# A feed-forward matrix cut into input halves for two blocks at once, and modulation sums moved between TensorE and VectorE

## The chip, the cores and the metric

One core of one Trainium2 chip. The metric is the device time of one execution in microseconds; the kernel before takes 1133.08 us (median of 3 runs, 1132.43 to 1134.42). Engines: TensorE (PE; PEld is its weight load), VectorE (DVE), ScalarE (ACT), GpSimd (POOL), and SP, whose queue issues most DMA loads.

## The reference

One layer of an encoder: 256 tokens, width 2048, float32.

```
mod = silu(c) @ mod_w + mod_b                  # six vectors of 2048: shift, scale, gate, twice
h   = x * (1 + scale_m) + shift_m
y   = windowed attention (32 heads of 64, 8 key heads) of h, then @ w_o
x   = layer_norm(alpha * x + (1 + gate_m) * y)
h   = x * (1 + scale_f) + shift_f
y   = square(relu(h @ w1 + b1)) @ w2 + b2      # w1 is 2048 x 8192, w2 is 8192 x 2048
out = layer_norm(alpha * x + (1 + gate_f) * y)
```

All weights are read once, so 1 MB tiles of weights stream in for the whole time.

## The kernel before

**Stream.** Every weight tile (128x2048) goes through one queue, `S`. `S.plan` appends a tile to the list, `loads` (L182) issues its DMA on SP as soon as one of five buffers (`raw`) is free, and `pump` works the tiles off in the order of the list. A matrix tile is cut into two halves of 128x1024; of each half ScalarE makes a rounded copy `wh` (L218, "high part") and VectorE the rest `wl` (L190, "low part"), five buffers each. TensorE multiplies high by high, high by low and low by high, so that the product has float32 precision from three fast passes (helper `mm3`, L439 to L441, for attention output and second feed-forward matrix).

**Modulation.** A vector of 2048 for one token, `silu(c) @ mod_w`, is a sum over weight tiles ("chunks"). The class `Mod` sums a chunk either on TensorE (`quad`, L274: 16 records for a chunk of a group of four columns, `raw` against `cact`) or on VectorE (L304, L306: two multiply-adds of 128x1024 into a part tile); which chunks go to VectorE is a list given for each `Mod`. At the end `quad` gathers VectorE's part on TensorE (L274 with `onesf`). The feed-forward shift and scale come as four groups of eight chunks, `m_ff` (tensor `modf`): group g serves the columns 512g to 512g + 511 of the feed-forward input. The attention gate is `m_gm`, the feed-forward gate `m_gf` (16 chunks of `modgf`, all on VectorE). `ff_columns(g)` turns a finished group into scale and shift (transposes L326 on TensorE, then small VectorE operations); `ff_input(g)` transposes the normed x (L834), and ScalarE (L840, L843) and VectorE (L846 and, for the low halves, L848) make the input group `h2[g]` of it, 512 rows of the transposed input.

**Order.** Where modulation chunks stand among the matrix tiles is written by hand: `SLOT_FILL` for the attention stage, `S.vecs(4)` at its end, `W1_FILL` among the tiles of the first feed-forward matrix. Within an engine, the order of instructions is chosen when the program is built, from the kernel's text and the free buffers; the engines then run their queues in that order.

**Hand-over.** At the end of attention, `project` makes the last columns of the output, `add_gated` (L688 to L690) adds them to x and collects statistics, `norm_scalars` (L694 to L704, with the square root on ScalarE, L698) and `normed` (L717, L719) apply the layer norm; then `ff_columns(0)`, `S.vecs(4)` and `ff_input(0)`.

**Feed-forward.** The 8192 hidden columns are four blocks (`BLK`). For block 0 the first matrix comes in tiles of 512 input rows by 512 hidden columns (`w1a`), in the order W1A: first the input groups 0 and 1 for all four column groups `fq`, then groups 2 and 3, with half sums parked in `uacc`; so it can start when only group 0 of the input exists. Its matmuls are 128x256 (L904 to L906). For blocks 1 to 3 `ff_hidden` takes a tile with all 2048 input rows for 128 hidden columns (`w1b`), with one 128x512 and one 128x256 matmul for a weight tile (L928, L929). After each block `ff_out` multiplies by the block's rows of the second matrix (`w2`) and adds to `ys`. The tiles of `m_gf` are planned among `w1b` and `w2` of block 1. During block 1, alpha times the norm's gain and bias is worked into x (`xs`), which stays in SBUF throughout. The general pool `gen` has 26 tiles of 128x1024.

Of the kernel before, what the change touches and what calls it, by code (L numbers as in the profile page):

```python
# [11 lines left out]
F32 = mybir.dt.float32  # L12
F32R = mybir.dt.float32r
# [7 lines left out]
S = 256  # L21
# [3 lines left out]
FF = 8192  # L25
# [5 lines left out]
BLK = 4  # L31
MIXG = (2, 4, 4, 4, 2)
FFG = (4, 4, 4, 4)
# [8 lines left out]
def hybrid_kernel(ctx: ExitStack, tc: tile.TileContext, a, out: bass.AP):  # L42
    nc = tc.nc
# [3 lines left out]
    whp = ctx.enter_context(tc.tile_pool(name="whp", bufs=NHIGH))  # L47
    wlp = ctx.enter_context(tc.tile_pool(name="wlp", bufs=NLOW))
    gen = ctx.enter_context(tc.tile_pool(name="gen", bufs=26))
    psa = ctx.enter_context(tc.tile_pool(name="psa", bufs=5, space=PSUM))  # L50
# [199 lines left out]
    S = Stream()  # L250
# [112 lines left out]
    m_gf = Mod([a["modgf"][i] for i in range(NK)], 512, range(NK), a["modgfb"])  # L363

# [12 lines left out]
    for g in range(G):  # L377
        n = MIXG[g] * 6 // 4
# [5 lines left out]
        for x, c in enumerate(chs):  # L384
# [4 lines left out]
            if not g:  # L389
                m_mix[1][0].plan(m)  # L390
            qk_order.append((g, c))
    late = [m_gm] + [m[0] for m in m_ff[:3]]
    lp = [0]

    def plan_late(n):
# [3 lines left out]
            if lp[0] < len(late):  # L399
                late[lp[0]].plan()  # L400

    W1_FILL = [1, 1, 1, 0, 0, 2, 0, 3, 0, 0, 0, 0, 0, 0, 0, 0]
    SLOT_FILL = dict(enumerate([0, 1, 2, 1, 0, 1, 3, 0, 1, 3, 2, 0, 3, 5, 1, 1, 3, 2, 1, 3, 0, 0, 1], -2))
    for n in range(-2, 21):
        plan_late(SLOT_FILL.get(n, 0))
        if n + 2 < len(LATE):
# [3 lines left out]
            S.plan(a["wo"][(n - 5) % 4, (n - 5) // 4])  # L410
    S.stop = len(S.q)
    plan_late(4)
    W1A = [(kg, fq) for p in ((0, 1), (2, 3)) for q in ((0, 1), (2, 3)) for kg in p for fq in q]
    for n, (kg, fq) in enumerate(W1A):
        left = [m.n - m.planned for m, _, _ in m_ff]
        for _ in range(max(W1_FILL[n], left[2] if n == 6 else 0, left[2] + left[3] if n == 8 else 0)):
            m_ff[2 if m_ff[2][0].planned < m_ff[2][0].n else 3][0].plan()
        S.plan(a["w1a"][kg, fq])
    NF = FF // 128 // BLK
    for blk in range(BLK):  # L420
        for f in range(NF):
            if blk:
                if blk == 1 and f % 2:
                    m_gf.plan()
                S.plan(a["w1b"][(blk - 1) * NF + f])
        for c in range(4):
            for kg in range(4):
                if blk == 1 and kg % 2:
                    m_gf.plan()
                S.plan(a["w2"][blk, c, kg], None, blk == BLK - 1 and c == 3 and kg > 1)  # L430


    acc, xts, held, xs = {}, {}, {}, []
# [1 line left out]
    def part(tiles, t, c):  # L435
        return tiles[c][:, t * 512:t * 512 + 512]
# [272 lines left out]
    def normed(c, t):  # L709
        mv, rstd = sc[t]  # L710
        z = part(xs, t, c)
        if t and c == 0:
            nm = sml.tile([128, 1], F32, name="nmr")
            nc.vector.scalar_tensor_tensor(nm, mv[:, 0:1], -1.0, rstd, op0=OP.mult, op1=OP.mult)
            sc.append(nm)
        if t:
            nc.scalar.activation(z, z, AF.Identity, scale=rstd, bias=sc[2])  # L717
        else:
            nc.vector.tensor_scalar(z, z, mv[:, 0:1], rstd, op0=OP.subtract, op1=OP.mult)  # L719
# [131 lines left out]
    def ff_in(k):  # L851

        return h2[k // 4][k % 4 // 2][:, k % 2 * 512:k % 2 * 512 + 512]

    h2 = [ff_input(0)]
    for c in range(1, 4):
        for t in range(NT):
            normed(c, t)


    def square_split(ps, ft, n, u, at):
# [20 lines left out]
        nc.vector.tensor_sub(l, uf, f32(h))  # L882

    g2 = None
    uacc = [g4() for _ in range(4)]
    us = []
    opened = {}
    for n, (kg, fq) in enumerate(W1A):
        if n in (1, 7, 9):
            ff_columns(len(h2))  # L890
            h2.append(ff_input(len(h2)))
        wh, wl = S.main()
        for fp in range(2):
            if kg % 2 == 0:
                opened[fq, fp] = psa.tile([128, 512], F32, name="pa")
            ps = opened[fq, fp]
            for fi in range(2):
                o = ps[:, fi * 256:fi * 256 + 256]
                for k in range(4):
                    w = (fp * 2 + fi) * 4 + k  # L900
                    hb = ff_in(4 * kg + k)
                    hh, hl = hb[:, :256], hb[:, 256:]
                    new, end = kg % 2 == 0 and fi + k == 0, kg % 2 == 1 and fi == 1 and k == 3
                    nc.tensor.matmul(o, wh(w, 128), hh, start=new, stop=False)  # L904
                    nc.tensor.matmul(o, wh(w, 128), hl, start=False, stop=False)  # L905
                    nc.tensor.matmul(o, wl(w, 128), hh, start=False, stop=end)  # L906
            S.done()
            av = uacc[fq][:, fp * 512:fp * 512 + 512]
            if kg == 1:
                nc.scalar.copy(av, ps)  # L910
            elif kg == 3:
                nc.vector.tensor_add(av, av, ps)
                u = g4(F32R)
                square_split(av, fq * 4 + fp * 2, 2, u, 0)
                us.append(u)

    def ff_hidden(blk):
        nonlocal g2
# [26 lines left out]
    def ff_out(blk, us, c):  # L945
# [6 lines left out]
                S.done()  # L952
        return pss

    ys = [g4() for _ in range(4)]
    bf = bias_all(a["b2"])
    for blk in range(BLK - 1):
        if blk:
            us = ff_hidden(blk)
        for c in range(4):  # L960
            if blk == 1:
                gb = [sml.tile([128, 512], F32, name="gb", tag="t2", bufs=4) for _ in range(2)]
                for n in range(2):
                    nc.gpsimd.dma_start(gb[n], a["lnrow"][n:n + 1, c * 512:c * 512 + 512].partition_broadcast(128))
            for t, ps in enumerate(ff_out(blk, us, c)):
                if blk == 0:
                    nc.vector.tensor_add(part(ys, t, c), ps, bf(c))
                else:
                    nc.vector.tensor_add(part(ys, t, c), part(ys, t, c), ps)
            if blk == 1:  # L970
# [47 lines left out]
def _layout(i):  # L1018
# [43 lines left out]
    n0 = FF // BLK  # L1062
    wa = w1[:, :n0].reshape(4, 4, 128, 4, 4, 128)
    o["w1a"] = cc(wa.transpose(0, 3, 2, 4, 1, 5).reshape(4, 4, 128, 2048))
# [28 lines left out]
```

## Time and profile before

| | before |
|---|---|
| median of 3 runs | 1133.08 us |
| the profiled execution | 1131.72 us, of which the span from first to last instruction is 1130.0 us |
| granted TensorE clock, mean | 0.994 |
| moved by DMA | 288.50 MB |
| hand-over: last matmul of attention to first of the first matrix | 388.18 to 396.64 us |
| first matrix of block 0 | 396.64 to 496.36 us |
| second matrix of block 0 | 496.5 to 583.4 us |
| blocks 1 to 3 | 583.5 us to the end |

All times in rows are microseconds from the start of the span. "L274" is line 274 of the kernel before; a row of the timeline has start, duration, engine, line, operation, output and inputs, shape and count, and in brackets how long the engine stood idle before and what ended it.

### The profile page before, as it was taken

Reading aid. Unit: us, or ns where it says so; the run is one execution under the profiler, and the core shown is the slowest. Engines: PE = TensorE matmul, PEld = TensorE weight load, DVE = VectorE, ACT = ScalarE, POOL = GpSimd, SP = SyncE. Lnnn points to the kernel's source line nnn. Section 1 sums busy time; section 2 is a strip of 40 time slices with the busy share of each in tenths; the row PEclk is TensorE's granted clock in tenths of the full one; section 3 lists DMA queues with packets and bytes.
Section 4 is the critical chain, followed back from the end, with each engine's and each line's share of the span. In section 5 each row is a group of like instructions: output and inputs, shape, how many; then the busy total and the mean of one; then the engine's idle time right before and its main releaser. Section 6 shows DMA issues by size and latency. Waiting matters only on the chain.

```text
span 1130.0 us, 15722 instructions
## 1 busy us (share of the span) xinstructions
PE 1091.6 (97%) x6224; PEld 876.6 (78%) x6224; DVE 810.1 (72%) x1123; ACT 539.3 (48%) x841; POOL 28.9 (3%) x47
## 2 busy tenths in 40 slices
PE   4899999999999999999999999999999999999995
PEld 2566677666676799998888888888888888888884
DVE  5556878987989977865568887966665656665576
ACT  2242345786676264753344543335454334444340
POOL 2000000000000000000000001020000000000001
PEclk9999999999999999999999999999999999999998
DMA  9998988876886599655577788775555557555522
GB/s 349 389 381 327 362 318 324 311 258 250 314 319 234 222 377 368 229 185 194 202 278 282 271 284 306 288 258 204 186 187 190 195 202 269 187 187 186 186 75 75
DMA packets 43866, 288.50 MB, mean 255 GB/s; under 512 B 5232, under 2 KB 7440, under 8 KB 10000
## 3 DMA queue, kind: packets, MB, share of 16 engines
q1 hardware_dynamic: 40640, 279.82, 67.5%
q0 software_dynamic: 2304, 6.36, 1.8%
q10 hardware_dynamic: 848, 1.31, 0.3%
q8 instruction: 49, 0.80, 0.3%
q14 instruction: 25, 0.20, 0.0%
HBM read 285.37 MB, written 2.10 MB: 254 GB/s over the span
## 4 chain that ended last, share of the span: by engine, by line
PE 91%; DVE 4%; DMA 3%; ACT 1%; issue 1%; DVEq 0%; ACTq 0%
PE pa L440 16%; PE pa L441 16%; PE pa L439 16%; PE pa L928 16%; PE pa L929 8%; PE pm L274 4%; PE pa L905 3%; PE pa L904 3%; PE pa L906 3%; DMA raw<-in_wqkv 2%; PE pa L680 2%; PE pt L665 1%; DVE wl L190 1%; PE pa L626 1%; PE pt L594 1%; DVE g L306 1%
## 5 line engine op out<-in xcount | busy, mean ns | idle before, releaser
L190 DVE TENSOR_TENSOR wl<-raw,wh 128x1024 fp32r<-128x1024 f32 x332 | 405.6, 1228 | 219.4 <-ACT wh L218 218.8
L218 ACT CAST wh<-raw 128x1024 fp32r<-128x1024 f32 x332 | 347.7, 1053 | 441.9 <-PE pa L441 232.9
L439 PE MATMUL pa<-wh,g 128*128 128x512 f32 x816 | 322.7, 397 | 4.0 <-ACT wh L218 4.0
L440 PE MATMUL pa<-wl,g 128*128 128x512 f32 x816 | 321.2, 394 | 2.8 <-DVE wl L190 2.8
L441 PE MATMUL pa<-wh,g 128*128 128x512 f32 x816 | 320.4, 393 | 0.0
L928 PE MATMUL pa<-g,wh 128*128 128x512 f32 x768 | 270.1, 396 | 0.0
L929 PE MATMUL pa<-g,wl 128*128 128x256 f32 x768 | 215.5, 281 | 0.0
L439 PEld LDWEIGHTS pa<-wh,g 128*128 128x128 f32 x816 | 153.6, 189 | 45.0 <-issue 6.5
L440 PEld LDWEIGHTS pa<-wl,g 128*128 128x128 f32 x816 | 154.2, 189 | 37.3 <-DVE wl L190 4.4
L441 PEld LDWEIGHTS pa<-wh,g 128*128 128x128 f32 x816 | 154.0, 189 | 35.7 <-issue 3.5
L928 PEld LDWEIGHTS pa<-g,wh 128*128 128x128 f32 x768 | 144.1, 188 | 34.6
L929 PEld LDWEIGHTS pa<-g,wl 128*128 128x128 f32 x768 | 145.1, 189 | 0.2
L306 DVE SCALAR_TENSOR_TENSOR g<-raw,cact,g 128x1024 f32<-128x1024 f32 (+1 forms) x83 | 100.6, 1216 | 9.4 <-DMA raw<-in_modgf 6.2
L905 PE MATMUL pa<-g,wh 128*128 128x256 f32 x256 | 72.7, 285 | 0.4 <-DVE g L848 0.4
L904 PE MATMUL pa<-g,wh 128*128 128x256 f32 x256 | 72.5, 286 | 0.0
L906 PE MATMUL pa<-g,wl 128*128 128x256 f32 x256 | 72.3, 283 | 0.0
L274 PE MATMUL pm<-raw,cact 128*32 128x256 f32 (+2 forms) x800 | 59.2, 406 | 8.9 <-DMA raw<-in_modm 7.9
L904 PEld LDWEIGHTS pa<-g,wh 128*128 128x128 f32 x256 | 48.8, 192 | 1.3 <-issue 0.8
L905 PEld LDWEIGHTS pa<-g,wh 128*128 128x128 f32 x256 | 49.1, 192 | 0.9 <-DVE g L848 0.8
L512 DVE TENSOR_TENSOR g<-g,pa 128x512 f32<-128x512 f32 x44 | 29.8, 682 | 27.0 <-PE pa L441 27.0
L906 PEld LDWEIGHTS pa<-g,wl 128*128 128x128 f32 x256 | 49.1, 192 | 0.0
L274 PEld LDWEIGHTS pm<-raw,cact 128*32 128x32 f32 x800 | 22.6, 114 | 32.7 <-issue 13.8
(169 smaller groups left out, 801.7 us busy)
## 6 DMA issues: line engine op xcount, KB each, us to landing
raw<-in_w SPq DMA_DIRECT2D x64, 1024.0 KB, 5.0
raw<-in_w1b SPq DMA_DIRECT2D x48, 1024.0 KB, 4.9
raw<-in_modm SPq DMA_DIRECT2D x32, 1024.0 KB, 8.1
raw<-in_modf SPq DMA_DIRECT2D x32, 1024.0 KB, 7.1
raw<-in_wqkv SPq DMA_DIRECT2D x24, 1024.0 KB, 7.1
raw<-in_modgm SPq DMA_DIRECT2D x16, 1024.0 KB, 5.3
raw<-in_wo SPq DMA_DIRECT2D x16, 1024.0 KB, 6.9
raw<-in_w1a SPq DMA_DIRECT2D x16, 1024.0 KB, 8.1
```

The lines of the kernel that those rows point to most:

```text
L190: nc.vector.tensor_sub(l, r, f32(self.hs[n]))
L218: nc.scalar.copy(h, s)
L274: nc.tensor.matmul(self.ps[32 * j:32 * j + 32, :w], lhsT, rhs[j], start=self.first, stop=stop)
L306: nc.vector.scalar_tensor_tensor(p[:, :e], s, cact[:, kt:kt + 1], p[:, :e], op0=OP.mult, op1=OP.add)
L439: nc.tensor.matmul(ps, xh, wh, start=start, stop=False)
L440: nc.tensor.matmul(ps, xh, wl, start=False, stop=False)
L441: nc.tensor.matmul(ps, xl, wh, start=False, stop=stop)
L904: nc.tensor.matmul(o, wh(w, 128), hh, start=new, stop=False)
L905: nc.tensor.matmul(o, wh(w, 128), hl, start=False, stop=False)
L906: nc.tensor.matmul(o, wl(w, 128), hh, start=False, stop=end)
L928: nc.tensor.matmul(ps, wh(k, 128), hb, start=k == 0, stop=False)
L929: nc.tensor.matmul(ps[:, :256], wl(k, 128), hb[:, :256], start=False, stop=k == NK - 1)
```

## The change

1. The first matrix of blocks 0 and 1 is now cut by input halves together: `w1a` covers 4096 hidden columns (8 column groups). A first pass does input groups 0 and 1 for all eight, then come groups 2 and 3 for block 0, its second matrix, groups 2 and 3 for block 1, its second matrix. `ff_hidden` remains for blocks 2 and 3.
2. The chunks of `m_ff` that VectorE sums: group 0 from (1, 5, 7) to (1, 4, 6), group 1 from (1, 4, 5, 6) to (0, 1, 2), group 2 from (2) to all, group 3 from (1, 2, 4, 5, 6, 7) to all. The four chunks at the end of attention are now the last of group 1, all on TensorE; groups 2 and 3 are planned within the first pass.
3. x is written to device memory by GpSimd's queue after the norm (`spill`) and read back ahead of the second matrix of block 2, and its four tiles go back to the pool in between; the work on x that stood in block 1 moves to block 2.
4. The bias `b2` comes column by column instead of as two tiles, and the tiles of `m_gf` are planned among `w2` of blocks 0 and 1.

```diff
-    m_ff = groups(a["modf"], FFG, [(1, 5, 7), (1, 4, 5, 6), (2,), (1, 2, 4, 5, 6, 7)])
+    m_ff = groups(a["modf"], FFG, [(1, 4, 6), (0, 1, 2), range(8), range(8)])
...
-    late = [m_gm] + [m[0] for m in m_ff[:3]]
+    late = [m_gm] + [m[0] for m in m_ff[:2]]
...
-    W1_FILL = [1, 1, 1, 0, 0, 2, 0, 3, 0, 0, 0, 0, 0, 0, 0, 0]
-    SLOT_FILL = dict(enumerate([0, 1, 2, 1, 0, 1, 3, 0, 1, 3, 2, 0, 3, 5, 1, 1, 3, 2, 1, 3, 0, 0, 1], -2))
+    SLOT_FILL = dict(enumerate([0, 1, 1, 1, 1, 1, 2, 1, 1, 2, 1, 1, 2, 2, 1, 1, 2, 1, 1, 2, 1, 1, 1], -2))
...
+    W1P = [[(kg, fq) for q in qs for kg in p for fq in (q, q + 1)]
+           for p, qs in [((0, 1), (0, 2, 4, 6)), ((2, 3), (0, 2)), ((2, 3), (4, 6))]]
+    W1_FILL = [0, 0, 1, 1, 1, 2, 1, 2, 1, 1, 2, 1, 1, 1, 1, 0]
+
+    def plan_ff():
+        def first(p):
+            for n, (kg, fq) in enumerate(W1P[p]):
+                for _ in range(0 if p else W1_FILL[n]):
+                    m_ff[2 if m_ff[2][0].planned < m_ff[2][0].n else 3][0].plan()
+                S.plan(a["w1a"][kg, fq])
+
+        def second(blk):
+            for c in range(4):
+                for kg in range(4):
+                    if blk < 2 and kg % 2:
+                        m_gf.plan()
+                    S.plan(a["w2"][blk, c, kg], None, blk == BLK - 1 and c == 3 and kg > 1)
...
+    z_far = far.tile([128, 4096], F32, name="z_far")
+
+    def spill(c):
+        nc.gpsimd.dma_start(z_far[:, c * 1024:c * 1024 + 1024], xs[c])
...
     h2 = [ff_input(0)]
+    spill(0)
     for c in range(1, 4):
         for t in range(NT):
             normed(c, t)
+        spill(c)
...
-    for n, (kg, fq) in enumerate(W1A):
-        if n in (1, 7, 9):
-            ff_columns(len(h2))
-            h2.append(ff_input(len(h2)))
...
+    def ff_first(p):
+        us = []
+        for n, (kg, fq) in enumerate(W1P[p]):
+            if p == 0 and n in (1, 9, 15):
+                ff_columns(len(h2))
+                h2.append(ff_input(len(h2)))
...
+    ff_first(0)
...
-            us = ff_hidden(blk)
+        us = ff_hidden(blk) if blk == 2 else ff_first(1 + blk)
+        if blk == 2:
+            xs = [g4() for _ in range(4)]
+            for c in range(4):
+                nc.gpsimd.dma_start(xs[c], z_far[:, c * 1024:c * 1024 + 1024])
```

The body of `ff_first` is otherwise that of the loop over W1A in before. The layout of `w1` in memory follows.

More of the change, by code (lines that the diff above doesn't have):

```diff
@@ L49, in hybrid_kernel @@
     gen = ctx.enter_context(tc.tile_pool(name="gen", bufs=26))
+    far = ctx.enter_context(tc.tile_pool(name="far", bufs=1, space=bass.MemoryType.DRAM))
     psa = ctx.enter_context(tc.tile_pool(name="psa", bufs=5, space=PSUM))
@@ L412, in hybrid_kernel @@
     plan_late(4)
-    W1A = [(kg, fq) for p in ((0, 1), (2, 3)) for q in ((0, 1), (2, 3)) for kg in p for fq in q]
-    for n, (kg, fq) in enumerate(W1A):
[L415 to L418, printed above, removed]
-    NF = FF // 128 // BLK
[L420 to L430, printed above, removed]
+    NF = FF // 128 // BLK
+    W1P = [[(kg, fq) for q in qs for kg in p for fq in (q, q + 1)]
[13 more added lines that the diff above has]
+                    S.plan(a["w2"][blk, c, kg], None, blk == BLK - 1 and c == 3 and kg > 1)
+        first(0)
+        for blk in range(BLK):
+            if blk < 2:
+                first(1 + blk)
+            else:
+                for f in range(NF):
+                    S.plan(a["w1b"][(blk - 2) * NF + f])
+            second(blk)
+    plan_ff()
     acc, xts, held, xs = {}, {}, {}, []
@@ L884, in hybrid_kernel @@
     g2 = None
[L885 to L888, printed above, removed]
-        if n in (1, 7, 9):
-            ff_columns(len(h2))
-            h2.append(ff_input(len(h2)))
[L892 to L915, printed above, removed]
@@ L1061, in _layout @@
     w1 = f(i["mlp_w1"])[0]
-    n0 = FF // BLK
-    wa = w1[:, :n0].reshape(4, 4, 128, 4, 4, 128)
-    o["w1a"] = cc(wa.transpose(0, 3, 2, 4, 1, 5).reshape(4, 4, 128, 2048))
+    n0 = FF // 2
+    wa = w1[:, :n0].reshape(4, 4, 128, 8, 4, 128)
+    o["w1a"] = cc(wa.transpose(0, 3, 2, 4, 1, 5).reshape(4, 8, 128, 2048))
     wb = w1[:, n0:].reshape(NK, 128, (FF - n0) // 128, 128)
```

43 lines of the change are left out of this document (35 added, 8 removed).

## The prediction

> **What bounds the kernel now.** I read the page first: busy shares, slices, chain.
>
> ```profile
> PE 1091.6 (97%) x6224; PEld 876.6 (78%) x6224; DVE 810.1 (72%) x1123; ACT 539.3 (48%) x841; POOL 28.9 (3%) x47
> ...
> PE   4899999999999999999999999999999999999995
> ...
> PE 91%; DVE 4%; DMA 3%; ACT 1%; issue 1%; DVEq 0%; ACTq 0%
> ```
>
> TensorE is busy in every slice but the ends and holds 91% of the chain. Next, the waits of TensorE: what ended its idle times, with total, count and longest.
>
> ```profile
> PE pm L274 <- DMA raw<-in_modm: 7.9, 2, 7.4
> ...
> PE pa L439 <- ACT wh L218: 4.0, 3, 2.8
> ...
> PE pm L274 <- DMA raw<-in_modf: 1.0, 1, 1.0
> PE pa L905 <- DVE g L848: 0.4, 1, 0.4
> ```
>
> The first two lie at the start and in the projection of the first 160 us, which the change leaves alone. The last two lie at the hand-over from attention to the feed-forward part, and are small. Then windows of the stages that the change touches (columns: stretch, length, busy PE, PEld, DVE, ACT, POOL, granted clock, DMA share, GB/s):
>
> ```profile
> 240.00:260.00 20.00, 20.00 (x101) 13.30 (x101) 19.00 (x35) 17.61 (x44) 0.00 (x0) 1.00 0.70 256
> ...
> 396.50:450.00 53.50, 53.11 (x453) 50.30 (x451) 41.76 (x56) 29.36 (x43) 0.00 (x0) 1.00 0.95 371
> 496.50:583.40 86.90, 86.90 (x386) 71.97 (x385) 49.50 (x49) 35.59 (x36) 0.00 (x0) 1.00 0.62 215
> ...
> 674.00:762.00 88.00, 88.00 (x392) 72.90 (x391) 69.41 (x71) 35.30 (x35) 12.73 (x15) 1.00 0.79 284
> ```
>
> TensorE is full even where VectorE is busy 19.00 of 20 us. So an instruction taken from TensorE here is worth its whole slot, and one that makes TensorE wait costs its whole wait.
>
> **The change, part by part.** First what TensorE saves and gains. The rows give a modulation chunk among matmuls, a group's gather of its VectorE part (L274 from onesf), and the two forms of the first matrix.
>
> ```profile
> 401.70 0.28 PE L906 MATMUL pa<-g,wl 128*128 128x256 f32 x1
> 401.91 1.07 PE L274 MATMUL pm<-raw,cact 128*32 128x256 f32 x16
> 402.91 0.39 PE L904 MATMUL pa<-g,wh 128*128 128x256 f32 x1
> 403.13 0.28 PE L905 MATMUL pa<-g,wh 128*128 128x256 f32 x1
> ...
> 444.66 0.64 PE L274 MATMUL pm<-g,onesf 128*32 128x256 f32 x8
> ...
> 464.19 0.28 PE L905 MATMUL pa<-g,wh 128*128 128x256 f32 x1
> ...
> 488.19 0.28 PE L904 MATMUL pa<-g,wh 128*128 128x256 f32 x1
> ...
> 583.54 0.39 PE L928 MATMUL pa<-g,wh 128*128 128x512 f32 x1
> ...
> 654.19 0.40 PE L928 MATMUL pa<-g,wh 128*128 128x512 f32 x1
> ```
>
> From 464.19 to 488.19 lie 200 matmuls: 0.120 us each. From 401.70 to 403.13 lie two of them and a chunk: 1.43 - 0.24 = 1.19 us. From 583.54 to 654.19 lie 200 pairs (L928, L929): 0.353 us each.
>
> Feed-forward chunks on TensorE fall from 18 (groups 0 to 3: 5, 4, 7, 2) to 10 (5, 5, 0, 0). Where they stand matters. Before stood 11 ahead of the last column of the attention output, 5 at the hand-over, 2 in the first matrix; in the built changed program 6, 4 and none.
>
> - Ahead of the hand-over: five chunks fewer. Alone they cost 1.19; next to transposes, which share the change of form, about the 1.00 from 401.91 to 402.91. I take 1.1: -5.5 us. Group 1's gather moves from here into the hand-over: -0.6. Sum **-6.1** (bounds -5.6, -6.6).
> - In the first matrix: one chunk leaves the part that I count below as hand-over, one the rest (-1.2); the rest has two gathers instead of one (+0.65). Sum **-0.55**.
> - Block 1 by halves: 256 x (3 x 0.120 - 0.353) = **+1.7**.
>
> **The hand-over** is where I differ from "fewer instructions, less time". After the last column of the attention output comes the layer norm, then the first input group; TensorE has only modulation chunks to do. Rows of before, its own clock:
>
> ```profile
> 378.26 0.33 SPq L182 DMA_DIRECT2D raw<-in_w1a  x1
> ...
> 382.74 0.39 PE L441 MATMUL pa<-wh,g 128*128 128x512 f32 x1
> ...
> 383.11 2.00 ACT L218 CAST wh<-raw 128x1024 fp32r<-128x1024 f32 x2 [7.05 <-DMA raw<-in_w1a]
> ...
> 385.13 1.28 ACT L698 ACT_TABLE_LOAD   x1
> ...
> 389.02 0.68 DVE L688 TENSOR_TENSOR tmp<-pa,g 128x512 f32<-128x512 f32 x1
> 389.63 0.68 DVE L690 BATCH_NORM_STATS2 st<-g 128x6 f32<-128x512 f32 x1
> ...
> 391.29 0.20 ACT L698 ACTIVATE sd<-ve 128x1 f32<-128x1 f32 x1 [4.88 <-DVE ve L696]
> ...
> 392.60 0.21 DVE L700 RECIPROCAL r<-sd 128x1 f32<-128x1 f32 x2
> 393.44 0.54 DVE L719 TENSOR_SCALAR g<-g,mv,r 128x512 f32<-128x512 f32 x1
> 394.08 1.52 ACT L717 ACTIVATE g<-g,nmr,r 128x512 f32<-128x512 f32 x2 [1.50 <-DVE nmr L714]
> 395.86 0.57 ACT L840 ACTIVATE g<-pt,b,a 128x256 fp32r<-128x256 f32 x1 [0.25 <-PE pt L834]
> 396.46 0.54 DVE L846 TENSOR_SCALAR g<-pt,a,b 128x256 f32<-128x256 f32 x1 [1.04 <-ACT g L840]
> ...
> 399.58 0.42 DVE L848 TENSOR_TENSOR g<-g,g 128x256 fp32r<-128x256 f32 x1
> ...
> 399.98 0.39 ACT L318 COPY mrow<-pm 128x256 f32<-128x256 f32 x1
> ...
> 415.04 0.28 PE L904 MATMUL pa<-g,wh 128*128 128x256 f32 x1
> ```
>
> In before the first w1a tile is requested at 378.26 and split by ScalarE at 383.11, long ahead of the table load and the square roots. In the built changed program it takes the buffer of the last output-projection tile, and VectorE's low part that frees this buffer has moved ten places back: behind the products of the third column, whose last matmul is that at 382.74. So, aligned there: the column's first half ends six matmuls of 0.353 - 0.120 = 0.23 earlier, at 382.74 + 0.39 - 1.4 = 381.8; from then VectorE does six operations at 0.61 each (389.02 to 389.63), then the low part (1.22), to 386.7; the load goes out, and lands 4.85 later (378.26 to 383.11), 391.55. ScalarE's queue has this tile's cast ahead of table load and roots: 391.55 + 1.05 + 1.28 + 2 x 0.2 = 394.3. The reciprocals start there instead of 392.60. Then ScalarE has group 1's row copy (0.39) and two casts (1.05 each) ahead of its norms, which start at 396.8 instead of 394.08; the first input activation at 398.3 instead of 395.86.
>
> VectorE, the norms done at 396.9, has two low parts ahead of the input group (2.45, to 399.4) and two products of group 2's modulation between its operations. The last low half of the input (399.58 in before) ends at 404.5 instead of 400.0. For what follows these groups are needed (minimum, median, maximum in ns):
>
> ```profile
> L218 ACT CAST wh<-raw x332: 1028/1053/1098, 20.8 to 1093.0; 128x1024 fp32r<-128x1024 f32 x166
> L190 DVE TENSOR_TENSOR wl<-raw,wh x332: 1193/1224/3419, 21.9 to 1094.1; 128x1024 fp32r<-128x1024 f32 x166
> L306 DVE SCALAR_TENSOR_TENSOR g<-raw,cact,g x83: 744/1279/1286, 14.0 to 754.1; 128x1024 f32<-128x1024 f32 x73, 128x512 f32<-128x512 f32 x10
> ```
>
> From 404.5 VectorE's queue holds, up to the last low half of the second input group, six low parts, four modulation products (1.21 each back to back), two 0.54, four 0.42 and six small ones (some 0.1 each, by the reciprocals' 0.21 for two): 7.3 + 4.85 + 1.1 + 1.7 + 0.6 = 15.6, to 420.1. TensorE has 75 matmuls on group 0 left (9.0) and eight transposes (some 0.7, by the gather's 0.64 for eight), is done at 414.3 and waits some 2.5 us. It passes its 124th matmul of the first matrix at 420.2; before passed it at 415.04, with a modulation chunk done besides. **+5.2**. Bounds: +1.7, the delay of the roots alone, if the rest of VectorE's queue finds cover; +8.5, if the load takes the usual 8.1 of this group:
>
> ```profile
> raw<-in_w1a SPq DMA_DIRECT2D x16, 1024.0 KB, 8.1
> ```
>
> **After that.** VectorE in the 16 tiles of the first half-input pass: 32 low parts (39.2), 32 modulation products (38.9), three input groups (3 x (1.1 + 1.7 + 0.6) = 10.2): 88.3 in TensorE's 768 x 0.120 = 92.2 plus some 6 of transposes and gathers. It fits, as in 240 to 260, but the queue is served in order: the shift and scale of group 2 wait for TensorE's transposes, placed at matmul 432, and behind them stand three products, two scalings, two low halves and the low part for half-tile 20. I count 6 + 1.2 us of VectorE against 6.6 of TensorE: **+0.7** (bounds 0, 3).
>
> At nothing I cost: group gf's 16 loads, now in the second matrix of blocks 0 and 1. Block 0's stage (496.50 to 583.40) gets 8 x 2 x 1.21 = 19.4 more on VectorE, 69 of 87, which is what 674 to 762 has already with TensorE full. The copy of x to memory and back, 2 MB each way: nobody waits for the writing but the buffers, and reading starts a whole second-matrix column (22 us) before its use; without that cover a reload costs the 4.85 of a load. The bias rows by column are 128x512 loads issued 22 us ahead of use.
>
> **Sum:** -6.1 - 0.55 + 1.7 + 5.2 + 0.7 = +0.95 on the profiled execution's 1131.72 (span 1130.0 and 1.7 around it). That execution lies 1.36 under the median of the runs, 1133.08; I put the forecast against the median: 1133.08 + 0.95, **1134.0 us**. With the hand-over between +3 and +7, its own range is 1131.5 to 1137.
>
> **Rivals.**
> 1. *The hand-over costs little.* For it: in before, TensorE had 5 chunks there and waited only 1.0 + 0.4. Against it: ScalarE's and VectorE's queues are served in order, and the cast stands ahead of the roots. At +1.7, and no hold at group 2: 1133.08 - 4.95 + 1.7 = **1129.8**; with nothing lost there, 1128.1.
> 2. *Loads cannot feed the first pass* (the side of slower). Its 32 loads and the copy of x are 35.7 MB; at the 371 GB/s of 396.50 to 450.00 that is 96 us from 386.7, to 483, some 10 us ahead of the last half-tile's need at about 493. It decides below 336 GB/s; at 284 (the row 674 to 762, where the demand set it) it takes 126 us, 19 late, and at 310, 115 us: 9 late. Five buffers freed one by one by a VectorE that is itself 90% busy make the lower rates possible. At 8 us late: **1142**.
> 3. *The clock drops.* After the 2.8 us of idle among the waits on `wh` above the granted clock fell:
>
> ```profile
> 38.50:43.50 5.00, 4.58 (x12) 3.28 (x13) 4.78 (x4) 1.10 (x2) 0.00 (x0) 0.68 0.94 351
> ```
>
> That cost 5 x 0.32 = 1.6 us. In the changed hand-over TensorE has four chunks and a gather (some 4.5 us) after its last matmul and then little until 404.5, and idles again at 414.3; so up to two drops, 3.2: **1137.2**; the first drop would fall into a stretch that waits for VectorE anyway, which is why the sum leaves it out. [...]
>
> **Chances:** forecast 0.50, rival 1 0.22, rival 2 0.15, rival 3 0.13. A measurement here tells about 0.2% (2.3 us) from no change: under 1130.8 is faster, over 1135.3 slower. Rival 1 gives 0.19 of faster and 0.03 of same; the forecast 0.02, 0.33 and 0.15 of faster, same and slower; rivals 2 and 3 are slower but for 0.01. Faster 0.21, same 0.37, slower 0.42. Range: rival 1's low end to between rivals 3 and 2, 1128.5 to 1140.
>
> **What would show it.** TensorE's records: 8 x 16 fewer modulation matmuls, 256 more of the half form. The first cast of a w1a tile after, not before, the last column's products, waiting for its load; the table load behind it; the square roots some 1.7 us later against the last L441; TensorE waiting for the low halves of the input (the line that is L848 in before) for some us in all, where it was 0.4. If the sum of TensorE's waits after 160 us stays at 2, rival 1 holds. If waits for `raw` or the low parts appear between 430 and 490, rival 2 does. A granted clock under 0.9 after 390 is rival 3. The forecast is wrong if the hand-over, from the last L441 of attention to the 124th matmul, is not 3 to 7 us longer, or if a stage after the first matrix gains waits.

## The result, and the profile after

The changed kernel takes 1140.83 us (median of 4 runs, 1138.92 to 1142.26), the kernel before 1133.72 us over 4 runs shown with it: ratio 1.0063, 95% interval 1.0045 to 1.0081. It is slower by 7 us; forecast was +0.95, with a range that ended at 1140. The profiled execution of after took 1138.92 us, its span 1137.2, 7.2 more than the span of before, so the two traces can be laid side by side.

The page of after, the lines that answer to those of before (busy shares, TensorE by slices, chain):

```profile
PE 1088.8 (96%) x6352; PEld 890.1 (78%) x6352; DVE 827.7 (73%) x1115; ACT 542.3 (48%) x841; POOL 34.7 (3%) x57
...
PE   4899999999999899999999999999999999999995
...
PE 91%; DVE 3%; DMA 3%; ACT 2%; issue 1%; DVEq 0%; ACTq 0%
```

TensorE has 2.8 us less to do than before (1091.6) and the span is 7.2 longer: it stands idle 10 us more. The page hardly shows where. One slice of 28 us went from 9 to 8, and the chain looks as before. TensorE's waits tell it (line waited for, total, count, longest):

```profile
PE pa L452 <- ACT g L653: 4.5, 2, 2.4
...
PE pa L928 <- DVE g L861: 2.6, 2, 1.8
PE pt L847 <- DVE g L732: 2.2, 1, 2.2
...
PE pt L847 <- ACT g L730: 1.4, 1, 1.4
...
PE pa L927 <- ACT wh L219: 0.4, 1, 0.4
```

(Line numbers shift: after's are those of before plus 1, from `mm3` to the input groups plus 13. The first matrix, L904 to L906 in before, is L927 to L929 in after; the hidden pairs, L928 and L929 in before, are L952 and L953.) New are 4.5 us for `L653`, the exponentials of the attention scores, and 6.2 us at the hand-over (`L861`, `L732`, `L730`). Now the timeline of TensorE, at the marks that cut the span into stages:

```profile
239.98 0.50 PE L452 MATMUL pa<-wh,g 128*128 128x512 f32 x1 [2.43 <-ACT g L653]
...
354.73 0.50 PE L452 MATMUL pa<-wh,g 128*128 128x512 f32 x1 [2.06 <-ACT g L653]
...
380.70 0.39 PE L454 MATMUL pa<-wh,g 128*128 128x512 f32 x1
...
393.78 0.44 PE L847 MATMUL pt<-ident,g 128*128 128x128 f32 x2 [2.25 <-DVE g L732]
395.60 1.54 PE L847 MATMUL pt<-ident,g 128*128 128x128 f32 x6 [1.38 <-ACT g L730]
...
398.94 0.58 PE L928 MATMUL pa<-g,wh 128*128 128x256 f32 x1 [0.77 <-DVE g L861]
...
415.64 0.46 PE L928 MATMUL pa<-g,wh 128*128 128x256 f32 x1 [1.78 <-DVE g L861]
...
419.99 0.28 PE L928 MATMUL pa<-g,wh 128*128 128x256 f32 x1
...
501.75 0.28 PE L929 MATMUL pa<-g,wl 128*128 128x256 f32 x1
...
1124.14 0.39 PE L454 MATMUL pa<-g,g 128*128 128x512 f32 x1
```

The same marks in before (two of them stand in the prediction: the third column's last matmul at 382.74 and the 124th of the first matrix at 415.04):

```profile
496.36 0.28 PE L906 MATMUL pa<-g,wl 128*128 128x256 f32 x1
...
1117.04 0.39 PE L441 MATMUL pa<-g,g 128*128 128x512 f32 x1
```

After minus before: end of the third column -2.04; from there to the 124th matmul of the first matrix 39.29 instead of 32.30, **+6.99**; from there to the 768th matmul 81.76 instead of 81.32, +0.44; from there to the last matmul of `mm3` 622.39 instead of 620.68, **+1.71**. Sum +7.10. So nearly all that the forecast missed lies in two places: attention gave 2.0 instead of 6.1, and the hand-over took 7.0 instead of 5.2.

At the hand-over TensorE also ran at half clock for two stretches (stretch, length, busy PE, PEld, DVE, ACT, POOL, granted clock, DMA share, GB/s):

```profile
396.00:400.00 4.00, 3.21 (x13) 2.49 (x12) 3.52 (x7) 3.71 (x8) 2.01 (x4) 0.50 1.02 379
400.00:402.20 2.20, 2.20 (x13) 2.20 (x12) 2.20 (x5) 2.20 (x4) 0.00 (x0) 0.51 1.01 408
...
416.00:418.00 2.00, 2.00 (x11) 2.00 (x11) 2.00 (x4) 1.07 (x3) 0.00 (x0) 0.50 0.99 418
```

TensorE's waits in the hand-over are 6.4 us (the bracketed rows above from 393 on and one of 0.21) against 1.35 in before: +5.0. Two modulation chunks fewer stand between the two marks (64 of their records instead of 96; one of the two is before's chunk at 401.91): at 1.0 to 1.2 each, some -2.2. What is left of +6.99, some 4.2 us, is put down to the half clock. From 415.64 to 419.28 seventeen matmuls took 3.64 us, which at 0.120 each would be 2.04: the second drop cost 1.6. The first, 6.8 us long (0.51 from 395.3 to 402.2), has the rest.

What sets the order there, from the queues of SP, ScalarE and VectorE in after:

```profile
384.60 4.29 SPq L183 DMA_DIRECT2D raw<-in_w1a  x2
...
389.48 1.04 ACT L219 CAST wh<-raw 128x1024 fp32r<-128x1024 f32 x1 [15.20 <-DVE st L703]
390.54 1.28 ACT L711 ACT_TABLE_LOAD   x1
391.84 0.30 ACT L711 ACTIVATE sd<-ve 128x1 f32<-128x1 f32 x2
...
391.20 1.23 DVE L191 TENSOR_TENSOR wl<-raw,wh 128x1024 fp32r<-128x1024 f32 x1
392.34 0.22 DVE L713 RECIPROCAL r<-sd 128x1 f32<-128x1 f32 x2
...
401.77 0.42 DVE L861 TENSOR_TENSOR g<-g,g 128x256 fp32r<-128x256 f32 x1
...
413.98 1.28 DVE L307 SCALAR_TENSOR_TENSOR g<-raw,cact,g 128x1024 f32<-128x1024 f32 x1
415.17 0.76 DVE L861 TENSOR_TENSOR g<-g,g 128x256 fp32r<-128x256 f32 x2
```

The first w1a load goes out at 384.60 (378.26 in before). Its cast at 389.48 stands ahead of the table load and the square roots, its low part at 391.20 between the variance and the reciprocals. At 413.98 a product of group 2's modulation stands just ahead of the low half of the input for which TensorE waits until 415.64; VectorE itself had waited 1.00 us, until 411.11, for the load of another tile of that modulation.

### The profile page after: what moved, and what is told of

It is laid out like the page before. It is cut to its first block, busy times and chain, and to the rows that moved or that the text cites. A ratio compares the mean times of both kernels' runs of the same rounds, so it can differ in the third digit from the quotient of the medians.

```text
span 1137.2 us, 16019 instructions
## 1 busy us (share of the span) xinstructions
PE 1088.8 (96%) x6352; PEld 890.1 (78%) x6352; DVE 827.7 (73%) x1115; ACT 542.3 (48%) x841; POOL 34.7 (3%) x57
## 4 chain that ended last, share of the span: by engine, by line
PE 91%; DVE 3%; DMA 3%; ACT 2%; issue 1%; DVEq 0%; ACTq 0%
PE pa L453 17%; PE pa L454 17%; PE pa L452 17%; PE pa L952 10%; PE pa L953 5%; PE pa L929 5%; PE pa L928 5%; PE pa L927 5%; PE pm L275 4%; PE pa L693 1%; PE pt L678 1%; DMA raw<-in_wqkv 1%; DVE g L307 1%; DMA raw<-in_modf 1%; PE pa L639 1%; ACT wh L219 1%
## 5 line engine op out<-in xcount | busy, mean ns | idle before, releaser
L952 PE MATMUL pa<-g,wh 128*128 128x512 f32 x512 | 179.6, 395 | 0.0
L928 PE MATMUL pa<-g,wh 128*128 128x256 f32 x512 | 146.5, 287 | 2.6 <-DVE g L861 2.6
L927 PE MATMUL pa<-g,wh 128*128 128x256 f32 x512 | 145.9, 287 | 0.7 <-ACT wh L219 0.4
L929 PE MATMUL pa<-g,wl 128*128 128x256 f32 x512 | 145.7, 286 | 0.0
L953 PE MATMUL pa<-g,wl 128*128 128x256 f32 x512 | 143.6, 280 | 0.0
L307 DVE SCALAR_TENSOR_TENSOR g<-raw,cact,g 128x1024 f32<-128x1024 f32 (+1 forms) x99 | 122.8, 1247 | 14.4 <-DMA raw<-in_modgf 12.4
L952 PEld LDWEIGHTS pa<-g,wh 128*128 128x128 f32 x512 | 96.0, 188 | 22.7
L928 PEld LDWEIGHTS pa<-g,wh 128*128 128x128 f32 x512 | 99.5, 194 | 3.1 <-DVE g L861 3.0
L927 PEld LDWEIGHTS pa<-g,wh 128*128 128x128 f32 x512 | 99.1, 195 | 2.0 <-ACT g L853 0.8
L929 PEld LDWEIGHTS pa<-g,wl 128*128 128x128 f32 x512 | 99.3, 195 | 0.4 <-issue 0.4
L953 PEld LDWEIGHTS pa<-g,wl 128*128 128x128 f32 x512 | 96.7, 189 | 0.2
L275 PE MATMUL pm<-raw,cact 128*32 128x256 f32 (+2 forms) x672 | 50.2, 409 | 6.9 <-DMA raw<-in_modm 6.9
L275 PEld LDWEIGHTS pm<-raw,cact 128*32 128x32 f32 x672 | 18.8, 115 | 27.3 <-issue 13.7
```

The lines of the kernel that those rows point to most:

```text
L275: nc.tensor.matmul(self.ps[32 * j:32 * j + 32, :w], lhsT, rhs[j], start=self.first, stop=stop)
L307: nc.vector.scalar_tensor_tensor(p[:, :e], s, cact[:, kt:kt + 1], p[:, :e], op0=OP.mult, op1=OP.add)
L952: nc.tensor.matmul(ps, wh(k, 128), hb, start=k == 0, stop=False)
L953: nc.tensor.matmul(ps[:, :256], wl(k, 128), hb[:, :256], start=False, stop=k == NK - 1)
```

## The experiments

To compare stages across runs, each profiled execution is cut at three matmuls: the 528th of `mm3` (210.26 us in before, the end of the projection), the last of the third column, and the 124th of the first matrix; the last stage ends with the last matmul of `mm3`. Differences from before, in us, each from one execution; the ratio is to the kernel before on the same chip.

| run | median us | ratio (95% interval) | attention | hand-over | after it |
|---|---|---|---|---|---|
| after | 1140.83 | 1.0063 (1.0045 to 1.0081) | -1.8 | +7.0 | +2.1 |
| e1, old places of chunks | 1136.37 | 1.0027 (1.0017 to 1.0037) | -2.4 | +1.7 | +3.2 |
| e2, products two tiles later | 1142.15 | 1.0082 (1.0069 to 1.0095) | +1.3 | +3.7 | +5.9 |
| e3, matrix part alone | 1135.04 | 1.0019 (1.0009 to 1.0028) | 0.0 | +0.1 | +3.4 |
| e4, gaps filled | 1140.73 | 1.0068 (1.0053 to 1.0083) | +1.4 | +5.8 | +2.2 |
| e5, last slots empty | 1136.23 | 1.0020 (1.0010 to 1.0031) | -1.8 | +1.5 | +4.1 |
| e6, old places, products spread | 1133.24 | 0.9994 (0.9985 to 1.0002) | -2.5 | -0.2 | +4.0 |
| e7, e6 with gaps filled | 1132.01 | 0.9979 (0.9971 to 0.9988) | -2.4 | -0.1 | +1.3 |
| e8, before less five chunks | 1134.20 | 0.9999 (0.9990 to 1.0007) | -2.4 | +2.7 | +3.6 |
| e9, before less the scaling | 1132.66 | 0.9991 (0.9981 to 1.0000) | -1.3 | 0.0 | +3.1 |
| e10, e9 less five chunks | 1130.12 | 0.9976 (0.9965 to 0.9988) | -7.2 | +2.4 | +1.4 |
| e11, e7, one scaling on VectorE | 1136.08 | 1.0025 (1.0013 to 1.0037) | +1.0 | +0.2 | +1.3 |
| e12, e7, two scalings on VectorE | 1139.59 | 1.0057 (1.0038 to 1.0075) | +6.7 | +2.7 | +1.3 |

Three things blur single stages. Attention of e2 and e4 has the same two waits of TensorE as after, 2.4 and 2.1 us, but there the clock fell behind them:

```profile
240.00:245.00 5.00, 5.00 (x13) 2.31 (x13) 2.88 (x7) 1.75 (x7) 0.00 (x0) 0.66 0.52 165
355.00:360.00 5.00, 3.85 (x10) 3.03 (x11) 3.10 (x8) 4.78 (x16) 0.00 (x0) 0.66 0.95 383
```

These are e2's windows; in after's execution both stretches have 1.00. That is 5 x 0.34 = 1.7 us twice, and without it e2 and e4 stand near -2 like after. And in e3, e5, e6, e8 and e10 the pairs of block 2's hidden matmuls go out every 0.353 us, in the others every 0.347; that is some 1.4 us of the last column. And TensorE reaches the first mark between 0.6 us earlier (e7) and 2.9 us later (e10) than in before, with the order of before ahead of it in both.

**e1: the new list of slots.**

```diff
-    SLOT_FILL = ... [0, 1, 1, 1, 1, 1, 2, 1, 1, 2, 1, 1, 2, 2, 1, 1, 2, 1, 1, 2, 1, 1, 1]
+    SLOT_FILL = ... [0, 1, 2, 1, 0, 1, 3, 0, 1, 3, 2, 0, 3, 5, 1, 1, 3, 1, 0, 0, 0, 0, 0]
```

> The changed kernel with the list of chunks per attention slot of the kernel before, cut to the same sum of 28 (0,1,2,1,0,1,3,0,1,3,2,0,3,5,1,1,3,1,0,0,0,0,0). Theory A: the two new waits of TensorE in attention (2.4 and 2.1 us, for a score tile that ScalarE's exponentials free) come from where the new list puts the chunks; with the old places they are gone, the third column of the output projection ends some 4 us earlier than in the changed kernel, and the time falls from 1140.8 to about 1136.5. Rival B: any list with five chunks fewer lets TensorE run into ScalarE's exponentials; then waits of about 4 us in all stand at other score tiles and the time stays within 1139.5 to 1141.

The time, 1136.37, is the one that theory A gave, but not for its reason. The two waits went, and three others came; TensorE's rows of e1:

```profile
313.38 0.53 PE L607 MATMUL pt<-identr,g 128*128 128x128 f32 x4 [0.90 <-ACT g L609]
...
324.56 1.93 PE L693 MATMUL pa<-g,g 128*64 128x512 f32 x6 [0.74 <-ACT g L680]
...
328.58 1.65 PE L348 MATMUL pa<-g,pick 128*128 128x512 f32 x6 [1.06 <-ACT g L342]
```

All on ScalarE again, so attention won only 0.6, as theory B had it. What won was the hand-over, +1.7 instead of +7.0. The rows of SP and ScalarE in e1 show the difference from after:

```profile
376.01 0.33 SPq L183 DMA_DIRECT2D raw<-in_w1a  x1
...
381.07 2.01 ACT L219 CAST wh<-raw 128x1024 fp32r<-128x1024 f32 x2 [7.67 <-DMA raw<-in_w1a]
383.10 1.28 ACT L711 ACT_TABLE_LOAD   x1
```

With no chunk in the last slots the first w1a tile is loaded 8.6 us earlier and cast ahead of the norm, as in before.

**e2: group 2's products later.**

```diff
-    W1_FILL = [0, 0, 1, 1, 1, 2, 1, 2, 1, 1, 2, 1, 1, 1, 1, 0]
+    W1_FILL = [0, 0, 0, 0, 1, 2, 1, 2, 1, 2, 1, 2, 1, 2, 1, 0]
-            if p == 0 and n in (1, 9, 15):
+            if p == 0 and n in (1, 11, 15):
```

> The changed kernel with group 2's products two tiles later in the first matrix (list 0,0,0,0,1,2,1,2,1,2,1,2,1,2,1,0; its scale and shift before tile 11 instead of 9). Theory A: VectorE's products stand in the chain to the second input group; without them the wait of 1.78 us at 415.64 and the clock drop behind it (1.6 us) go, the first low half comes earlier too, and the time falls by 2.5 to 4 us, to 1137 to 1138.3. Rival B: the products are only moved, VectorE is now late for the low parts of tiles 5 to 15, new waits of TensorE between 430 and 490 take the gain, and the time stays within 1140 to 1142. Rival C: the hand-over is lost to the late load and the clock, not to the products; under 1 us is won.

Both A and B: the hand-over is 3.3 us shorter (+3.7 for +7.0), and what follows 3.8 us longer. The longest of the waits there is for a low part that VectorE makes behind the products:

```profile
PE pa L929 <- DVE wl L191: 1.8, 1, 1.8
```

**e3: the matrix part alone.**

```diff
-    m_ff = groups(a["modf"], FFG, [(1, 4, 6), (0, 1, 2), range(8), range(8)])
+    m_ff = groups(a["modf"], FFG, [(1, 5, 7), (1, 4, 5, 6), (2,), (1, 2, 4, 5, 6, 7)])
-    late = [m_gm] + [m[0] for m in m_ff[:2]]
+    late = [m_gm] + [m[0] for m in m_ff[:3]]
-    SLOT_FILL = ... (the new list)
+    SLOT_FILL = ... (the list of before)
-    W1_FILL = [0, 0, 1, 1, 1, 2, 1, 2, 1, 1, 2, 1, 1, 1, 1, 0]
+    W1_FILL = [1, 1, 1, 0, 0, 2, 0, 3, 2, 0, 0, 0, 0, 0, 0, 0]
```

> The matrix part alone: first matrix by input halves for blocks 0 and 1, copy of x to memory and back, gf's loads in blocks 0 and 1, but the modulation lists, the late groups and the chunks per slot of the kernel before (its eight chunks of groups 2 and 3 that the first matrix takes stand at tiles 0 to 8 as 1,1,1,0,0,2,0,3,2; 18 feed-forward chunks on TensorE). Theory A: it costs the 1.7 us of block 1 by halves and next to nothing else: about 1.5 to 2.5 above the kernel before, 1135.2 to 1136.2; no wait above 1 us at the hand-over and the granted clock 1.00 there. Rival B: the copy of x or the loads cost too, and most of the loss of 7 us is the matrix part: 1139 to 1141.

Theory A: 1.8 us above before (1.0 to 3.2), nothing in attention or at the hand-over. Copying x out and back, the loads of `gf` and the bias by columns cost nothing that shows. So 5 of the 7 us belong to the modulation part. (Of the +3.4 in its last column, 1.4 are the slower pairs of block 2.)

**e4: the clock.**

```diff
+    def fill_te(n, src):
+        pd = psa.tile([128, 512], F32, name="pa")
+        for i in range(n):
+            nc.tensor.transpose(pd[:, :128], src, ident)
...
+    fill_te(18, ident)
     h2 = [ff_input(0)]
+    fill_te(8, part(xs, 0, 0)[:, :128])
...
+            if p == 0 and n == 2:
+                fill_te(14, ident)
```

> The changed kernel with transposes of the identity that nobody reads on TensorE in its idle gaps at the hand-over: 18 before the first input group's transposes, 8 between the first and second half of them, 14 before tile 2 of the first matrix (some 0.115 us each). Theory A: about 3 us of the hand-over's loss is TensorE at half clock after the gaps (granted clock 0.50 from 396 to 402 and from 416 to 419); with the gaps filled the clock stays at 1.00 from 390 to 420, the waits stay about as they are, and the time falls by 1.5 to 3 us, to 1138 to 1139.3. Rival B: VectorE's queue sets the pace there, a faster TensorE only waits longer for it, and the time stays within 1140.2 to 1141.5.

Rival B. The clock stayed at 1.00 up to 400, TensorE then ran into VectorE, and the drop came later. The windows of e4:

```profile
396.00:400.00 4.00, 3.29 (x27) 2.57 (x25) 4.00 (x13) 3.85 (x6) 0.83 (x2) 1.00 1.01 428
400.00:405.00 5.00, 3.23 (x15) 3.03 (x16) 5.00 (x10) 5.00 (x9) 1.31 (x3) 0.67 0.98 365
```

The hand-over got 1.2 us shorter, the median did not move. The half clock came with the waits, and filling these three gaps moved it (0.57 from 401 to 409) rather than took it away.

**e5: the late load.**

```diff
-    SLOT_FILL = ... 1, 1, 2, 2, 1, 1, 2, 1, 1, 2, 1, 1, 1]
+    SLOT_FILL = ... 1, 1, 2, 2, 1, 1, 2, 2, 2, 3, 0, 0, 0]
```

> The changed kernel with the chunks of the last three attention slots moved two to four slots ahead (end of the list 2,2,2,3,0,0,0 for 2,1,1,2,1,1,1); all earlier places stay. After the first runs: the list with the old places won some 5 us, but only 0.6 of it ahead of the third column of the output projection (three other waits, 2.9 us in all, came for the two that went) and 4.1 between the last matmul of attention and the 124th of the first matrix, where the first w1a tile was now cast at 381, ahead of the table load. Theory A: the late chunks hold the buffers, so that w1a's first load goes out behind the last low part; with slots 18 to 20 empty it goes out before 380, the stretch from the last matmul of attention to the 124th of the first matrix falls from 32.4 to about 28.5 us, while the wait at 240 stays, and the time is about 1137. Rival B: the hand-over got better in that run because TensorE came 2 us earlier to it, not by the load; then it stays above 31 us and the time above 1139.5.

Theory A: the load goes out 6.4 us earlier, the hand-over falls to +1.5, and the median by 4.6 us, with the first wait in attention still there. From e5's queues of TensorE and SP:

```profile
241.64 0.50 PE L452 MATMUL pa<-wh,g 128*128 128x512 f32 x1 [2.44 <-ACT g L653]
...
378.25 0.33 SPq L183 DMA_DIRECT2D raw<-in_w1a  x1
```

Attention is as long as in after (-1.8). So the late load, not TensorE's lead, made the hand-over long.

**e6 and e7: the products spread, and the gaps filled.**

```diff
(on e1)
-    W1_FILL = [0, 0, 1, 1, 1, 2, 1, 2, 1, 1, 2, 1, 1, 1, 1, 0]
+    W1_FILL = [0, 0, 0, 1, 1, 1, 2, 2, 1, 1, 1, 1, 1, 1, 2, 1]
-            if p == 0 and n in (1, 9, 15):
+            if (p, n) in ((0, 1), (0, 11), (1, 0)):
(e7: with the filling of e4 besides)
```

> The list with the old places, and the products of groups 2 and 3 from tile 3 on, one chunk a tile (0,0,0,1,1,1,2,2,1,1,1,1,1,1,2,1), scale and shift of group 2 before tile 11, of group 3 before tile 16. Theory A: VectorE's products in the chain of the second input group and their crowding in tiles 5 to 11 cost what the run with the old places still loses in the first pass (1.5 us in the hand-over, 1.6 from the 124th to the 768th matmul); spread out they cost half of it or less, and the time falls from 1136.4 to 1134 to 1135. Rival B: as in the run with the products two tiles later, what is won at the hand-over is lost behind it, and the time stays within 1136 to 1138.

> As the run with the products spread, and the idle gaps of TensorE at the hand-over filled with transposes that nobody reads (18, 8 and 14). Theory A: the granted clock of 0.66 at 396 to 400 costs about 1.3 us of TensorE that no wait takes back once VectorE's queue is free of products there; with the gaps filled the clock stays at 1.00 and the time is 1 to 1.5 us under that of the run without them, 1133 to 1134. Rival B: as in the run with the gaps filled alone, TensorE only waits longer for VectorE; within 0.5 us of the run without them.

e6: theory A and a little more, 1133.24. The hand-over costs nothing now (-0.2); of the first pass one wait is left:

```profile
482.91 0.39 PE L929 MATMUL pa<-g,wl 128*128 128x256 f32 x1 [0.91 <-DVE wl L191]
```

e7 is the one version that beats both kernels, 1132.01, by 0.12 to 0.29%. But not by theory A's reason: the hand-over is the same as in e6 (-0.1 for -0.2), although the clock is 1.00 throughout (e6: 0.50 from 396.7 to 400.1). The difference, 2.7, lies after it, where the build of e7 has the faster pairs in block 2 (1.4) and no wait at 482.91 (0.9). That filling the gaps helps is not shown.

**e8: what five chunks are worth.**

```diff
(on before)
-                else:
+                elif i not in self.skip:
                     stop = last and k == kc - 1 and not self.dve and self.bias is None
...
+    for n, sk in enumerate([(4, 6), (0, 2), (0,)]):
+        m_ff[n][0].skip = sk
```

> The kernel before with five chunks of the feed-forward modulation left out on TensorE in attention (chunks 4 and 6 of group 0, 0 and 2 of group 1, 0 of group 2: their matmuls are not issued, so that the modulation is not that of the reference; their loads and all else stay). It measures the term that the forecast put at 1.1 us a chunk. Theory A: TensorE is full there, so each chunk is worth its slot: 5.5 us less, about 1128. Theory B, from the runs so far: without the chunks as cover TensorE runs into ScalarE's exponentials and casts; new waits of 2 to 4 us in attention, and only 1.5 to 3.5 us less, 1130 to 1131.7.

Theory B, and more than that. 5.5 us of matmuls are left out with nothing put in their place, and attention gets 2.4 shorter (lines of e8 are those of before plus 3 here):

```profile
304.08 1.23 PE L668 MATMUL pt<-ident,g 128*128 128x128 f32 x6 [0.90 <-ACT g L658]
...
311.62 1.02 PE L597 MATMUL pt<-identr,g 128*128 128x128 f32 x8 [0.57 <-ACT g L670]
...
313.54 0.53 PE L597 MATMUL pt<-identr,g 128*128 128x128 f32 x4 [0.91 <-ACT g L599]
...
392.93 0.68 PE L837 MATMUL pt<-ident,g 128*128 128x128 f32 x2 [2.20 <-DVE g L722]
```

Behind these waits the clock fell too, to 0.50 from 314.5 to 317.9. And what is won is given back: two low parts of w1a tiles now stand in VectorE's queue within the norm, and TensorE waits 2.20 at the hand-over. After it, this execution has a wait of 1.15 for a low part at 734 and the slower pairs. In the end the median does not move.

**e9 and e10: what TensorE runs into.**

```diff
(on before, in normalise)
-        for r in range(4):
+        for r in range(0):
(e10: with the chunks of e8 left out besides)
```

> The kernel before with the scaling of the probabilities by their sums left out on ScalarE (four instructions of 0.43 us for each of 16 score tiles; the attention output is then not that of the reference). By itself only the base for the next run: both theories expect no more than 1 us of difference, since TensorE waits only 0.3 us in attention in the kernel before.

> The same, and the five modulation chunks left out on TensorE in attention as in the earlier run (so neither modulation nor attention output is that of the reference). With ScalarE at its full work the five chunks were worth 2.4 us up to the end of attention instead of 5.5. Theory A: what takes the rest is ScalarE, whose exponentials, scalings and copies TensorE then waits for; with 1.7 us less of them in each slot the chunks are worth 4.5 to 5.5 us at the last matmul of attention, against the run with the scaling alone left out. Theory B: the order of VectorE's queue (mask, maximum, low parts) holds TensorE up; then they are worth 2 to 3 us again.

Attention is 1.3 us shorter in e9 and 7.2 in e10: without the scaling of the probabilities the five chunks are worth 6.0 us, all of their 5.5. Two waits are left, of 0.87 and 0.24 at 311 and 312. The 6.0 is the upper end: e10 came to the first mark 2.2 us later than e9, and counted from the start of the span the third column ends 3.8 us earlier (378.37 for 382.12), against 1.6 in e8 (381.09 for 382.74). Either way more than twice as much as with the scaling. The medians lie 2.5 us apart; the rest is given back at the hand-over (+2.4).

**e11 and e12: ScalarE's load, or the chain.**

```diff
(on e7, in normalise)
-            if r < 0:
+            if r < 1:        (e12: r < 2)
                 nc.vector.tensor_scalar(v, v, rs[:, r:r + 1], None, op0=OP.mult)
```

> The kernel with the old places, the products spread and the gaps filled (1132.0 us), with one of the four scalings of each score tile on VectorE instead of ScalarE: 0.43 us a slot less for ScalarE, about 0.5 more for VectorE (a 128x256 TENSOR_SCALAR row took 0.54). Theory A: ScalarE holds TensorE up in attention (with its scalings left out, five chunks were worth 6.0 us instead of 2.4); then the new waits of 3.1 us in attention fall to about 2.5, and the time to 1131 to 1131.7. Rival B: VectorE, 84% busy there, hands the time back through its own queue; 1131.8 to 1133.

> The same with two of the four scalings on VectorE: 0.87 us a slot less for ScalarE, about 1 us more for VectorE. Theory A: waits in attention near 2 us or less, time 1130 to 1131.3. Rival B: VectorE becomes the one that holds TensorE up; waits for the mask, the low parts or the scaled probabilities, 1132 to 1135.

Rival B in both, worse than it said. ScalarE is relieved (93.05 us busy from 225 to 380 in e12, 105.29 in e7), and attention gets 3.4 and 9.1 us longer than in e7. TensorE still waits for ScalarE, for the copy of the turned probabilities behind the scaling; e12:

```profile
316.85 1.02 PE L607 MATMUL pt<-identr,g 128*128 128x128 f32 x8 [1.41 <-ACT g L680]
...
334.55 2.91 PE L693 MATMUL pa<-g,g 128*64 128x512 f32 x6 [2.54 <-ACT g L680]
```

So less work on ScalarE does not by itself shorten its part, as theory A had it; since VectorE got that work, these runs do not price the relief alone. What fits all of e8 to e12, but is only argued, is the chain of one score tile through three engines (mask and maximum on VectorE, exponentials and scaling on ScalarE, transposes on TensorE, copy on ScalarE, values): left out, the scaling makes it shorter; on VectorE it stands behind low parts and products. (Of e12's 9.1, up to 5 are the clock, 0.87 from 300 to 340.) How much of the chain each link has was not measured.

## Why the prediction was wrong, point by point

**Ahead of the hand-over, -6.1: this step failed.** "An instruction taken from TensorE here is worth its whole slot" was read from TensorE's 20.00 of 20 us busy. Busy showed that work was always there, not that what follows was ready. The chunks were the work that covered the chain of the score tiles. Measured up to the end of the third column: -1.8 in after, -2.4 in e8 where nothing is put in their place, and -6.0 for the same five chunks in e10 where the scaling is left out. The rows of before could have told, TensorE and ScalarE at the place of after's first wait:

```profile
237.66 1.06 PE L274 MATMUL pm<-raw,cact 128*32 128x512 f32 x8
...
237.71 0.48 ACT L640 ACTIVATE g<-pa,nm 128x256 f32<-128x256 f32 x1 [2.53 <-DVE nm L634]
...
238.78 0.50 PE L439 MATMUL pa<-wh,g 128*128 128x512 f32 x1
```

The exponentials that free the buffer for the matmul at 238.78 started at 237.71, and the chunk at 237.66 filled just that time; without it the matmul waits. (This chunk is one of the attention gate's, by its eight 128x512 records; the new list has none on TensorE at this place.) In after the exponentials start later besides:

```profile
238.91 0.47 ACT L653 ACTIVATE g<-pa,nm 128x256 f32<-128x256 f32 x1 [3.91 <-DVE nm L647]
```

There a low part and a product stand between mask and maximum in VectorE's queue. Costing a removal needs the slack of the next instruction, not the share of busy time.

**The hand-over, +5.2 (bounds +1.7, +8.5): mechanism right, size 1.8 too small.** The forecast's times are laid at the third column's last matmul, which stands 2.04 us earlier in after; with 2.04 added, after's rows follow them closely. The first load goes out at 386.6 (forecast 386.7), its cast starts at 391.5, ahead of table load and square roots (391.55), the reciprocals at 394.4 (394.3); the last low half of the first input group ends at 404.2 (404.5), that of the second at 420.2 (420.1). What failed is the step behind it: that waits for VectorE would hide the clock's drops, so that the sum may leave them out. TensorE runs out of work at 415.9 (forecast 414.3), waits 1.78 (2.5), does its next 17 matmuls at half clock (1.6 more), and passes the 124th at 422.0 instead of 420.2. e5 shows that the late load is the bulk of the +7.0 (7.0 to 1.5), e6 that the products in the chain are the rest (1.7 in e1, -0.2 in e6).

**The rest of the first matrix, -0.55 + 0.7 = +0.15:** +0.44, with one wait of 0.44. **Block 1 by halves, +1.7:** +1.71. **At nothing:** the copy of x, the bias columns and the loads of `gf` cost nothing that shows (e3).

**Rivals.** Rival 1 (hand-over cheap, 1129.8): its reading of the hand-over is what e6 reaches by another order, but without the -6.1 that gives 1133.2. Rival 2 (loads): TensorE has no wait for `raw` or low parts between 430 and 490 in after. Rival 3 (clock, 3.2 us): both drops are there, at some 4.2 in the trace, and what the hand-over took beyond the forecast, 1.8, is part of that; but with the gaps filled only 1.2 came back in e4 and nothing in e7 against e6.

**The range** took the hand-over's bounds in full and gave the -6.1 only 0.5 either way. The term that looked safest came out between 1.8 and 6.0 for the same five chunks, by what else stood in the stage.

## What to carry to other kernels

An engine that is busy all the time may be so because filler work was put where it would wait; before counting a removal as gain, look for the instruction behind it and when its operands were ready. At a hand-over, follow the buffer that lets the next stage's first load go out, and what stands between it and the stage's first dependent instruction in each engine's queue. A list that interleaves small work is a schedule: change its amounts and its places in separate steps, and measure stages, since a total that fits can come from somewhere else (e1).

## What the runs showed of the hardware that was not expected

- The same wait of 2.4 us of TensorE was followed by full clock in one execution (after, 1.00 from 240 to 245) and by a drop in two others (0.66 in e2 and e4). After's four runs, spread over 3.3 us, fit that: the longer, the lower the mean clock (0.989 to 0.985). No wait of after behind the first 25 us was longer than 2.8 us, and the 1.78 us ahead of 415.64 were followed by 0.50 from 415.81 to 419.22. In the clock records of before and after, the stretches at half clock between 30 and 1100 us are 3.41 us long (from 40.27 and 67.57 in before, from 40.34, 67.64 and 415.81 in after) but for one of 6.83 (from 395.32 in after). In the 3.41 us just ahead of 395.32 and of 415.81 TensorE was idle for 2.97 and 2.00; in those just ahead of 239.98 it was idle for 2.43, and the clock stayed at 1.00; ahead of 67.64 it was busy for all of the 7.64 us from 60.00 on, at 1.00, and the clock fell. So the idle time just ahead does not by itself tell when the clock falls; what does is not shown.
- At half clock, from 415.8 to 419.2, a matmul of the first matrix took 0.213 us instead of 0.120.
- Pairs of hidden matmuls go out every 0.353 us in some blocks and every 0.347 in others of the same kernel (in before 0.353 from 583.54 and from 953.17 on, 0.347 from 779.19 on), at granted clock 1.00 and with no wait; in block 2 it differs between builds. Two rows of after in block 2, 100 pairs apart, 34.67 us:

```profile
791.83 0.39 PE L952 MATMUL pa<-g,wh 128*128 128x512 f32 x1
...
826.50 0.39 PE L952 MATMUL pa<-g,wh 128*128 128x512 f32 x1
```

And of e3, 100 pairs apart, 35.33 us:

```profile
787.42 0.40 PE L952 MATMUL pa<-g,wh 128*128 128x512 f32 x1
...
822.75 0.40 PE L952 MATMUL pa<-g,wh 128*128 128x512 f32 x1
```

  Over a block of 256 pairs this is 1.4 to 1.7 us, as much as the price of block 1 by halves. Why it is so stays open.
- Leaving five matmul chunks out changed the built order well behind them: in e8 VectorE's differs from before up to 415 us and TensorE's up to 458. From there on all queues hold the same order as in before, so the wait at 734 and the slower pairs of block 2 in e8 don't come from it. At 730.74 VectorE waits 2.91 us for a load of `modgf` (2.48 at the same place in before, where TensorE did not have to wait).
